# Soft mixture-of-experts on one core: products of one kind paired in every phase, and twenty-five pairs split a level deeper in place of nine

## The chip, the core and the metric

The kernel runs on one NeuronCore of a Trainium2 chip. The metric is the device time of one execution in microseconds (us). The profile is of one execution of the program; "span" is the time from its first to its last instruction in that profile, and the profiled execution's own time lies a little above it.

## The reference, cut to what matters

```python
# x (16, 512, 512), router_logits (16, 512, 8), expert_weights (8, 512, 2048), all f32
probs = softmax(router_logits, axis=-1)
for e in range(8):
    output += probs[:, :, e:e+1] * np.matmul(x, expert_weights[e])
```

With 8192 rows in all, this is one matrix product: on the left the 8 scaled copies of x side by side (8192 x 4096), on the right the experts' weights below each other (4096 x 2048).

## The kernel before, in words

**A fast product.** The kernel doesn't do the eight multiplications that a 2 x 2 by 2 x 2 block product has, but Winograd's seven, at two levels, and in some places three. At the outer level the rows go in blocks of 256; blocks a = 2q and b = 2q + 1 are a pair (q = 0 to 15), the experts are halved (0 to 3, 4 to 7) and the output's columns are halved (1024 each). This gives the seven products P1, P2, P5, P6, P7, P4 and P3, each for every q: `product(r, q)`. Each multiplies a left operand of 256 rows (some sum of x scaled by routing probabilities, made on VectorE by `times` and `less` in class `Left`) by a right operand (some sum of weight blocks, class `Right`), and adds the result into quarters of the output. `P1`, `P2` and `PQ` also name the three sets of probabilities in `p_dram`: first half of the experts, second half, and their sum.

At the inner level each product is again seven steps, `STEPS = (1, 5, 6, 2, 7, 3, 4)`. A step (`Product.step`) is 8 matmuls of 128 x 128 weights by 512 columns in float16 into a PSUM bank; `Product.post` then moves or adds the bank into f32 tiles `h` of 128 x 512 and sends a finished one out with a DMA. `post_alone` starts a result with ScalarE copies. `post_on_base` adds to a base, a tile read in beforehand: VectorE adds in six of the seven steps, ScalarE copies in step 2. Four h tiles make up the result of one product. The pool `hpool` has twelve, which also hold the `t5` copies below.

**A third level.** `run_third` does steps 1 and 5 of both products of a stage together, as seven parts each (class `Third`: sums `s` of the two left operands, made on VectorE; class `Split`: sums `t` of the right operand, made once, eight for the two steps). A part is 4 matmuls of 256 columns. So 56 matmuls of 256 columns stand in place of 32 of 512. After part 5 ScalarE copies half a bank to another bank and the other half to an h tile `t5` (L638 and L640), in that order, first for step 1 and then for step 5; VectorE adds `t5` back in parts 6 and 7. The last two steps of the stage before are held back and put between the parts (`held`).

**Stages.** `add` makes a stage of two products (the single (6, 0) and the last are alone). A stage has 14 slots, the steps of the two products by turns. There are 56 stages, 0 to 55: 0 to 3 have two P1 each; 4 to 9 one P2 and one P1; 10 to 14 two P2; 15 two P5; 16 to 30 P6 with P5; 31 is (6, 15) with (7, 0); 32 to 46 are P4 with P7; 47 is (4, 15) with (3, 0); 48 to 54 two P3; 55 the last P3. `k5`, `k7` and `k3` are 15, 31 and 47. Split are stages 2 and 3 (P1), 11 (P2), and 49 to 54 (P3).

**What sets the order.** All engines' instructions are kept in the order in which the Python code emits them. Hooks (`at(stage, slot, ...)`) put DMAs and weight work at a slot. VectorE's tasks wait in `queue`; `slack` runs them by a planner with two clocks, a slot of 1.73 us for TensorE (`SLOT`) and a cost for each task (0.69, 1.22 or 2.29 us), as far as VectorE's clock stays under TensorE's by `LAG`. `need` forces a task early when a step asks for it. `start_loads`, `store_loads` and `finish_loads` bring x and the probabilities for two stages later, at slots 1, 5 and 7; `late` moves the first for one stage.

**Queues.** SP's queue loads bases (`Base.fetch`), x and the probabilities, transposes x (L397), and stores x. POOL's queue casts weights and x from f32 (`cast_w`, `XBlock.begin`), writes results (`to_out`; for P4 and P3 with an accumulating DMA, `accum_op=ADD`), and stores made weights. ACT's queue, in order with ScalarE's copies, loads weights (`fetch_w`) and kept left operands (class `Operand`). Weight tiles are 1 MB; `wpool` has fifteen, which also hold the sums `s` and `t` and the operands.

**Bases and operands.** P6's left operand is stored for q in `KEEP` (1 to 13) and read again as a part of P3's. P7 makes its own from both x blocks (three passes for each half). P7 reads as its base what P6 wrote to the output; P4 takes P7's result as its base while that is still in h tiles, which is why the two share a stage. P2 does the same with P1's for q of 9 and more, and reads P1's stored result for smaller q.

**Weights in time.** `cast21`, `wedge`, `cast_odd` and `odd_t` make the sums of weight blocks for P2, P5 and P6 during stages 0 to 15; `by_parts` makes those of P7, P4 and P3 in quarters and stores them; `turnover` loads the seven right operands of P7, P4 and P3 over the last slots before they are used.

Of the kernel before, what the change touches and what calls it, by code (L numbers as in the profile page):

```python
# [31 lines left out]
def kernel(  # L32
# [340 lines left out]
    def evacuated(cost=0.69):  # L373
        clock["dve"] = max(clock["dve"], clock["pe"]) + cost
# [51 lines left out]
    class Left:  # L426
# [31 lines left out]
        def queue_make(self, k):  # L458
            for make in self.makes(k):
                self.task[k] = later(1.22, make)  # L460

        def queue_s2(self):
# [3 lines left out]
            self.task["s2"] = later(0.69, make)  # L466

        def queue_i(self):
# [5 lines left out]
            self.task["i"] = later(1.22, make)  # L474
# [19 lines left out]
    class Right:  # L494
# [9 lines left out]
        def queue_sum(self, sums, p):  # L504
            self.task[p] = later(2.29, sums[p])
# [66 lines left out]
    class Split:  # L572


        def __init__(self, right):
            self.right, self.t, self.task = right, {}, {}

        def queue(self):
            for p in THIRD:
                for i in range(4):  # L580
                    self.task[p, i] = later(0.69, lambda p=p, i=i: self.make(p, i))
# [18 lines left out]
    class Third:  # L600


        def __init__(self, a, b, split):
            self.a, self.b, self.split, self.task, self.s, self.t5 = a, b, split, [], None, {}

        def queue_sums(self):
            for i in range(4):
                self.task.append(later(0.69, lambda i=i: self.make(i)))

        def make(self, i):  # L610
            if i == 0:
                self.s = wpool.tile([P, 4, C, HQ], f16, name="s", tag="w")
            s, (a, b) = self.s, (p.left.t[0] for p in (self.a, self.b))
# [12 lines left out]
        def part(self, p, m):  # L626
# [14 lines left out]
            elif m in (6, 7):  # L641
                evacuated(0.42)
# [41 lines left out]
    right[1] = Right(w, {p: Task(2.29, sums[p]) for p in (6, 7, 4)})  # L684
    lefts, xs, ps_, bases = {}, {}, {}, {}
    KEEP = range(1, 14)
# [6 lines left out]
    def left_of(r, q, fresh=True):  # L693
# [15 lines left out]
        if r == 3 and q in KEEP:  # L709
            pt = PBlock(a, P2)  # L710
            return Left(xblock(a), pt, part=Operand(lefts[6, q].kept)), [xblock(a), pt]
# [6 lines left out]
    def product(r, q, **how):  # L718
# [7 lines left out]
        elif r == 2:  # L726
            if q >= 9:
# [21 lines left out]
        elif r == 4:  # L749
            p = Product(right[4], left, to_out(q, 1, 0, accum_op=ADD), products[7, q].o.__getitem__)  # L750
# [36 lines left out]
    def third(stage, r):  # L787
        if r not in splits:
            splits[r] = Split(right[r])
# [30 lines left out]
    def run_third(stage):  # L820
        t = thirds[stage]
        before(stage, 0)
        t.parts("x1", "x5", "q1", "q5")
# [4 lines left out]
        t.parts("x2", "q2", "x6", "q6")  # L828
# [4 lines left out]
        t.parts("x7", "q7", "x3", "q3", "x4", "q4")  # L833
        for p in THIRD:
            for product in (t.a, t.b):
                product.post(p)
        after(stage, 4)

    def run(stage):
# [3 lines left out]
        slots = [(p, i) for i in range(len(STEPS)) for p in some]  # L843
# [23 lines left out]
    for q in (2, 4, 6, 8):  # L867
        add(product(1, q), product(1, q + 1))
    for q in range(9, 15):
# [344 lines left out]
```

## Time and profile before

| | |
|---|---|
| runs, median (3) | 1382.1 us (1379.82 to 1384.07) |
| the profiled execution | 1378.23 us |
| its span | 1376.5 us |
| granted TensorE clock | 1.00 |
| VectorE busy | 1125.8 us, 1360 instructions |
| moved by DMA | 358.50 MB |

"A <- B: total, times, longest" tells who waited for whom. In the timeline a row is a run of equal instructions with its start, its length, and in brackets the idle time ahead of it and what ended that. In the view by stretches each engine has its busy time and count; the last three columns are the granted clock, the mean busy share of the sixteen DMA engines, and GB/s. The DMA share can be over 1, since packets overlap. A line number is often that of a helper: L132 is every matmul, L112 every VectorE sum, L123 SP's DMAs, L126 POOL's, L166 ACT's loads.

### The profile page before, as it was taken

The page shows a single profiled execution, that of the slowest core. Times are in us where ns is not written, and L with a number is a line of the kernel's source. Part 1 is how long each engine was busy: PE and PEld are TensorE (multiplying, and loading weights), DVE is VectorE, ACT ScalarE, POOL GpSimd, SP SyncE. Part 2 cuts the span into 40 slices and gives each one's busy share as a digit, 9 for nine tenths or more (in the row PEclk, how much of TensorE's full clock was granted, in tenths as well). Part 3 has the DMA queues.
Part 4 walks back from the last instruction along what each step waited for, and adds up shares of the span by engine and source line. Part 5 has one row for each costly group of instructions (what it writes and reads, how often), then busy time and mean ns, then how long its engine had stood idle before and what let it go on. Part 6 is the DMA issues. An engine that isn't in the chain of part 4 may idle for free.

```text
span 1376.5 us, 18061 instructions
## 1 busy us (share of the span) xinstructions
PE 1363.1 (99%) x6610; PEld 643.8 (47%) x6610; DVE 1125.8 (82%) x1360; ACT 193.3 (14%) x353; POOL 411.4 (30%) x652
## 2 busy tenths in 40 slices
PE   8999999999999999999999999999999999999998
PEld 4455444445444444444444444444444444456554
DVE  5877767678989888789897878888889898987875
ACT  3222111100001111111111100000000000123221
POOL 3122333231222243343242112232332422232222
PEclk9999999999999999999999999999999999999999
DMA  9999899999897999999999898888797969999886
GB/s 180 199 258 219 214 233 279 236 315 340 252 327 237 321 308 315 295 318 320 334 286 307 327 399 237 194 236 211 227 266 203 259 188 310 289 225 239 211 184 117
DMA packets 193161, 358.50 MB, mean 260 GB/s; under 512 B 53168, under 2 KB 87216, under 8 KB 187696
## 3 DMA queue, kind: packets, MB, share of 16 engines
q0 software_dynamic: 88688, 185.12, 55.7%
q1 hardware_dynamic: 98336, 130.15, 31.1%
q10 hardware_dynamic: 6048, 42.08, 8.0%
q8 instruction: 51, 0.84, 0.2%
q14 instruction: 38, 0.31, 0.1%
HBM read 214.47 MB, written 170.07 MB: 279 GB/s over the span
## 4 chain that ended last, share of the span: by engine, by line
PE 69%; issue 11%; DMA 11%; POOL 5%; DVE 3%; SPq 1%; ACT 0%; POOLq 0%; DVEq 0%; ACTq 0%
PE ps L132 69%; POOL out_dram L126 3%; DMA out_dram<-h 3%; DMA wd<-w 2%; DMA w<-in_expert_weights_dram 2%; DMA w<-wd 2%; DMA xT<-xs 1%; POOL wd L126 1%; DMA pT<-p_dram 1%; SPq L397 1%; DVE h L112 1%; POOL w L126 1%; DVE z L112 1%; DVE s L112 0%; POOL xs L126 0%
## 5 line engine op out<-in xcount | busy, mean ns | idle before, releaser
L132 PE MATMUL ps<-w,z 128*128 128x512 f16 (+1 forms) x5272 | 1136.0, 376 | 3.8 <-DMA w<-in_expert_weights_dram 1.9
L132 PEld LDWEIGHTS <-z 128*128 128x128 f16 x5344 | 522.6, 98 | 609.6 <-issue 2.5
L126 POOL DMA_DIRECT2D out_dram<-h x380 | 248.6, 660 | 724.1 <-ACT h L559 352.2
L112 DVE TENSOR_TENSOR h<-ps,h 128x512 f32<-128x512 f32 x415 | 284.7, 688 | 175.0 <-PE ps L132 147.0
L112 DVE TENSOR_TENSOR z<-xT,pT 128x2048 f16<-128x2048 f16 x220 | 266.8, 1218 | 12.1 <-DMA xT<-xs 10.0
L132 PE MATMUL ps<-w,d 128*128 128x512 f16 x880 | 199.1, 379 | 1.2 <-DMA w<-wd 1.2
L132 PEld LDWEIGHTS <-d 128*128 128x128 f16 x880 | 86.1, 98 | 103.3 <-issue 1.5
L112 DVE TENSOR_TENSOR z<-z,d 128x2048 f16<-128x2048 f16 x110 | 132.3, 1217 | 0.0
L112 DVE TENSOR_TENSOR w<-w 128x1024 f16<-128x1024 f16 (+2 forms) x92 | 101.0, 1103 | 5.9 <-DMA wd<-w 3.4
L559 ACT COPY h<-ps 128x512 f32<-128x512 f32 x64 | 37.5, 586 | 482.9 <-PE ps L132 414.2
L548 ACT COPY h<-ps 128x512 f32<-128x512 f32 x90 | 52.7, 586 | 325.6 <-PE ps L132 304.6
L112 DVE TENSOR_TENSOR ps<-ps,h 128x512 f32<-128x512 f32 (+1 forms) x102 | 60.6, 599 | 31.9 <-PE ps L132 31.8
L112 DVE TENSOR_TENSOR d<-z 128x1024 f16<-128x1024 f16 x110 | 74.8, 686 | 2.0 <-PE ps L132 0.7
L545 ACT COPY h<-ps 128x512 f32<-128x512 f32 x90 | 52.0, 589 | 151.7 <-PE ps L132 146.6
L126 POOL DMA_DIRECT2D w<-in_expert_weights_dram x65 | 48.4, 761 | 38.6 <-DMA wd<-w 28.3
L126 POOL DMA_DIRECT2D wd<-w x86 | 48.2, 584 | 37.1 <-DVE w L112 28.9
L126 POOL DMA_DIRECT2D kept<-h x56 | 30.8, 550 | 73.8 <-ACT h L548 41.1
L112 DVE TENSOR_TENSOR z<-z,u 128x2048 f16<-128x2048 f16 x38 | 46.4, 1221 | 0.6
L112 DVE TENSOR_TENSOR u<-xT,pT 128x2048 f16<-128x2048 f16 x38 | 46.3, 1217 | 0.0
L112 DVE TENSOR_TENSOR h<-h 128x512 f32<-128x512 f32 (+2 forms) x69 | 45.2, 676 | 0.4 <-DMA h<-kept 0.3
L541 ACT COPY ps<-ps 128x512 f32<-128x512 f32 x45 | 25.6, 570 | 104.5 <-PE ps L132 99.4
L112 DVE TENSOR_TENSOR z<-z 128x2048 f16<-128x2048 f16 x32 | 39.1, 1222 | 0.6
(61 smaller groups left out, 262.5 us busy)
## 6 DMA issues: line engine op xcount, KB each, us to landing
out_dram<-h POOLq DMA_DIRECT2D x380, 256.0 KB, 6.7
pT<-p_dram SPq DMA_DIRECT2D x127, 256.0 KB, 6.3
w<-wd ACTq DMA_DIRECT2D x27, 1024.0 KB, 9.4
h<-kept SPq DMA_DIRECT2D x100, 256.0 KB, 7.1
xT<-x SPq DMA_DIRECT2D x74, 256.0 KB, 6.6
wd<-w POOLq DMA_DIRECT2D x72, 256.0 KB, 6.7
w<-in_expert_weights_dram POOLq DMA_DIRECT2D x35, 512.0 KB, 9.9
h<-out_dram SPq DMA_DIRECT2D x68, 256.0 KB, 4.8
```

The lines of the kernel that those rows point to most:

```text
L112: dve(nc.vector.tensor_tensor(out=o, in0=a, in1=b, op=op))
L126: note(nc.gpsimd.dma_start(out=o, in_=i, **how))
L132: note(nc.tensor.matmul(ps, z, w, start=start, stop=stop, skip_group_check=True))
L397: note(nc.sync.dma_start_transpose(out=self.t[:, :, ds(j * P, P)], in_=self.xs[:, j, :]))
L541: act(nc.scalar.copy(self.banks["b"], x))
L545: act(nc.scalar.copy(o[tn], q if p == 5 else x))
L548: act(nc.scalar.copy(o[TN[p]], b if p == 2 else x))
L559: act(nc.scalar.copy(o[tn], b))
```

## The change

Products of one kind now stand in one stage together. Stages 0 to 6 have two P1 each, 7 to 14 two P2, 15 to 31 are as they were, 32 to 38 have two P7, 39 is (7, 15) with (4, 0), 40 to 46 have two P4, and the rest is as it was. `k2` is 7 and `k4` is 39. So P4's result can't find P7's in h tiles, and reads it back from the output; P2 reads P1's stored result for q up to 13. P7's left operand is x of block b times `P2` less P6's kept one, for q of 1 to 14 (`KEEP` is one longer). Split are 2 to 6 (P1), 8 to 11 (P2), 33 to 37 (P7, step 1 alone), 41 to 45 (P4), and 49 to 54 (P3) as before. The weights of P4 and P3 are loaded in the one stage before their first use, every second slot. Casts and sums of weights for P2, P5 and P6 get other slots, and block (1, 1) of P5's and P6's is made from whole casts. The loads of x and probabilities start at slot 6 in stages 32 to 46. The planner's costs are lowered. The last product does step 3 before 7 and step 2 in two halves around step 4, both copied by ScalarE.

```diff
-    def evacuated(cost=0.69):
+    def evacuated(cost=0.61):
...
-        def __init__(self, right):
-            self.right, self.t, self.task = right, {}, {}
+        def __init__(self, right, ps):
+            self.right, self.ps, self.t, self.task = right, ps, {}, {}
...
-    KEEP = range(1, 14)
+    KEEP = range(1, 15)
...
-        if r == 3 and q in KEEP:
-            pt = PBlock(a, P2)
-            return Left(xblock(a), pt, part=Operand(lefts[6, q].kept)), [xblock(a), pt]
+        if q in KEEP and (r == 7 or r == 3 and q < 14):
+            h = a if r == 3 else b
+            pt = PBlock(h, P2)
+            return Left(xblock(h), pt, part=Operand(lefts[6, q].kept)), [xblock(h), pt]
...
-            if q >= 9:
+            if q >= 14:
                 base = products[1, q].o.__getitem__
...
-            p = Product(right[4], left, to_out(q, 1, 0, accum_op=ADD), products[7, q].o.__getitem__)
+            base = bases[4, q] = Base(lambda tn: out_rows(q, 1, 1, tn))
+            p = Product(right[4], left, to_out(q, 1, 0, accum_op=ADD), base)
...
     def run_third(stage):
         t = thirds[stage]
+        both = len(t.split.ps) == 2
+        some = ("x1", "x5", "q1", "q5", "x2", "q2", "x6", "q6") if both else ("x1", "x5", "x2", "x6")
         before(stage, 0)
-        t.parts("x1", "x5", "q1", "q5")
+        t.parts(*some[:4] if both else some[:2])
...
-    for q in (2, 4, 6, 8):
+    for q in range(2, 16, 2):
         add(product(1, q), product(1, q + 1))
-    for q in range(9, 15):
-        add(product(2, q), product(1, q + 1))
...
-    rest = [15] + list(range(9))
-    for i in range(0, 10, 2):
+    rest = [14, 15] + list(range(14))
+    for i in range(0, 16, 2):
         k = add(product(2, rest[i]), product(2, rest[i + 1]))
...
-    for q in range(15):
-        add(product(4, q), product(7, q + 1))
+    for q in range(1, 15, 2):
+        add(product(7, q), product(7, q + 1))
+    some = product(7, 15)
+    xs.clear()
+    k4 = add(some, product(4, 0))
+    for q in range(1, 15, 2):
+        add(product(4, q), product(4, q + 1))
...
+    for stage in range(k7 + 1, k3):
+        late[stage] = 6
...
+    for r, first in ((7, k7 + 1), (4, k4 + 1)):
+        for slot, tn in zip((8, 10, 12, 13), INNER):
+            for q in range(16):
+                if (r, q) != (7, 0):
+                    k = first + (q - 1) // 2
+                    fetch_at(k if tn == (1, 0) else k - 1, 3 if tn == (1, 0) else slot, bases[r, q], tn)
...
-    for i, kn in enumerate(((0, 0), (0, 1), (1, 1), (1, 0))):
-        at((11 * i + 8) // 14, (11 * i + 8) % 14, lambda kn=kn: cast21(kn))
+    for where, kn in zip([(3, 10), (4, 7), (5, 4), (5, 13)], ((0, 0), (0, 1), (1, 1), (1, 0))):
+        at(*where, lambda kn=kn: cast21(kn))
...
+    for q, where in zip((12, 11, 22), [(7, 4), (7, 10), (8, 2), (8, 12)]):
+        at(*where, lambda q=q: cast_odd(q, (1, 1)))
+    at(*(8, 12), lambda: odd_t((1, 1)))
...
-    by_parts(k7 + 4, 4, 36, 3, cast_part(22), keep_raw, (9, 16))
+    by_parts(k7 + 2, 4, 36, 3, cast_part(22), keep_raw, (9, 16))
...
-    turnover(k7, 0, 4, "t4")
-    turnover(k3 - 1, 1, 3, "b22")
+    for r, raw, stage in ((4, "t4", k4 - 1), (3, "b22", k3 - 1)):
+        turnover_of(r, raw, [(stage, 1 + 2 * i) for i in range(7)])
...
-    finish.steps = (1, 5, 6, 7, 3, 4, 2)
+    finish.steps = (1, 5, 6, 3, 7, "2a", 4, "2b")
...
-    for stage in (2, 3):
+    for stage in [2, 3, 4, 5, 6]:
         third(stage, 1)
-    at(1, 2, splits[1].queue)
-    for stage in (11,):
+    at(1, 0, splits[1].queue)
+    for stage in [8, 9, 10, 11]:
         third(stage, 2)
-    at(10, 2, splits[2].queue)
+    at(k2, 2, splits[2].queue)
...
+        at(k7 - 1 + (q - 1) // 2, 8 + 3 * ((q - 1) % 2), lambda q=q: lefts[7, q].part.fetch())
...
+    for r, stages_ in ((7, [2, 3, 4, 5, 6]), (4, [2, 3, 4, 5, 6])):
+        for stage in stages_:
+            third((k7 if r == 7 else k4) + stage, r, *([(1,)] if r == 7 else []))
+        if stages_:
+            at((k7 if r == 7 else k4) + stages_[0] - 1, 2, splits[r].queue)
```

In the changed file the copies of the split stand at L639 and L641.

## The prediction

> **What bounds the kernel now.** I read the page first, then who TensorE waited for, then its timeline, then the transfers and VectorE by stage.
>
> ```profile
> span 1376.5 us, 18061 instructions
> PE 1363.1 (99%) x6610; PEld 643.8 (47%) x6610; DVE 1125.8 (82%) x1360; ACT 193.3 (14%) x353; POOL 411.4 (30%) x652
> ```
>
> TensorE is busy for 99% of the span. The profile calls that no proof of a full engine, since matmuls are pipelined, so I take the waits and the start-to-start times.
>
> ```profile
> PE ps L132 <- DMA w<-in_expert_weights_dram: 1.9, 1, 1.9
> PE ps L132 <- DVE h L112: 1.5, 2, 0.8
> PE ps L132 <- ACT h L331: 1.4, 1, 1.4
> PE every L94 <- DVE zero L91: 1.3, 1, 1.3
> PE ps L132 <- DVE t L112: 1.3, 1, 1.3
> PE ps L132 <- DMA w<-wd: 1.2, 1, 1.2
> PE ps L132 <- DVE s L112: 1.0, 1, 1.0
> PE ps L132 <- ACT ps L638: 0.3, 1, 0.3
> PE ps L132 <- DVE ps L112: 0.2, 1, 0.2
> ```
>
> Columns: us in total, times, longest. All of TensorE's waits come to 10.1 us. Those for expert weights, L331 and zero (4.6 us) lie in the prologue, which stays as it is. The rest is 5.5 us: 1.5 + 1.3 + 1.2 + 1.0 + 0.3 + 0.2. So the time is the sum of the matmuls, and only fewer matmul columns or fewer waits can shorten it.
>
> ```profile
> 198.97 14.41 PE L132 MATMUL ps<-w,z 128*128 128x512 f16 x66
> ...
> 1216.94 2.76 PE L132 MATMUL ps<-w,z 128*128 128x512 f16 x16
> ...
> 1240.32 2.76 PE L132 MATMUL ps<-w,z 128*128 128x512 f16 x16
> ```
>
> The columns are start, us, and how many in a row; the last matmul's pipeline adds about 0.16 us to each row. 66 matmuls of 512 columns take 14.41 us, or 0.216 us each. A stage of two unsplit products has 112 of them: 24.18 us. The other two rows mark the same place in two split stages that follow each other (49 and 50): 23.38 us for 80 matmuls of 512 and 56 of 256 columns. 80 x 0.2159 is 17.27, so one of 256 columns takes 0.109 us, half of the long one and 1 ns.
>
> **The change part by part.**
>
> *More split pairs.* A full split puts 56 short matmuls in place of 32 long ones: 24.18 - 23.38 = 0.80 us. Before has nine; after has twenty full ones (5 of P1, 4 of P2, 5 of P4, 6 of P3) and five of P7 that split step 1 alone: 28 short for 16 long, 3.45 - 3.06 = 0.40 us. Eleven more full and five half: 8.8 + 2.0 = **10.8 us less** on TensorE, on the path that sets the end.
>
> *Old waits.* P1's halves are queued two slots earlier (DVE ps and one DVE h); P2 and P1 no longer share stages 4 to 9, and stage 11 is no longer the first split of P2; P4's weights no longer wait for P6's tiles (DMA w<-wd); the next left operand of the last split is planned in time; the last product does step 3 before step 7. I let all **5.5 us** go, and then ask what is late next.
>
> *First splits on new bases.* In before the first P2 split stood still here:
>
> ```profile
> 308.75 0.60 PE L132 MATMUL ps<-t,s 128*128 128x256 f16 x4 [1.26 <-DVE t L112]
> 311.86 0.60 PE L132 MATMUL ps<-w,z 128*128 128x256 f16 x4 [0.35 <-ACT ps L638]
> ```
>
> Its eight weight combinations on VectorE came late. In after the stage ahead of the first split of P2 and of P4 (7 and 40) has 25.7 us of VectorE work for 25.9 us of TensorE, and that of P7 (32) 25.1 for 25.05. The rates are start to start:
>
> ```profile
> 195.19 2.35 DVE L112 TENSOR_TENSOR z<-xT,pT 128x2048 f16<-128x2048 f16 x2
> 197.47 0.68 DVE L112 TENSOR_TENSOR h<-ps,h 128x512 f32<-128x512 f32 x1
> 198.06 0.68 DVE L112 TENSOR_TENSOR d<-z 128x1024 f16<-128x1024 f16 x1
> 198.66 1.22 DVE L112 TENSOR_TENSOR z<-xT,pT 128x2048 f16<-128x2048 f16 x1
> ```
>
> They give 0.60 us for an eviction or a 1024-column sum and 1.13 for a 2048-column one. Three such places at 0 to 1.3 us; I take half: **1.9 us**.
>
> *The copy's tile.* The second wait is another thing. The split's ScalarE copy into `t5` needs an h tile, of which there are twelve, and a product with a base holds four. The tile was still being written out:
>
> ```profile
> 311.16 0.37 ACT L640 COPY h<-ps 128x256 f32<-128x256 f32 x1 [3.66 <-DMA out_dram<-h]
> ```
>
> ```profile
> 294.26 1.53 POOL L126 DMA_DIRECT2D w<-in_expert_weights_dram x2 [0.21 <-PE ps L132]
> 298.46 0.57 POOL L126 DMA_DIRECT2D out_dram<-h x1 [2.67 <-ACT h L559]
> ```
>
> ```profile
> 298.46 12.62 DMA out_dram<-h
> ```
>
> The write took 12.62 us behind two 512 KB casts in POOL's queue. ScalarE is in order, so the copy for the other half (L638), and with it TensorE, waited behind it. In after, P2's, P7's and P4's fourteen splits all have bases, and the same tile order: from the write of step 2 to the copy lie five steps and two parts, 5 x 1.73 + 0.87 = 9.5 us. The median write takes 6.7 us (last fence below), so most pass. Two have casts just ahead (slot 4 of stages 7 and 33, write in slot 6). Each costs between 0 and the 0.35 + 1.26 = 1.6 us that this one would have cost without the wait beside it: **3.2 us**; the other end is all nine full ones of P2 and P4, 14.4 us.
>
> *VectorE in P7.* Taking x_b P2 minus the kept operand saves one pass per k half, 28 x 1.13 = 32 us of VectorE over the phase. But P7 and P4 apart load it unevenly: a half-split P7 stage has 12 evictions (7.2), 10 wide sums (11.3), two s2 (1.2), four half sums (1.2), two short adds (0.7), plus about 1.2 of weight sums: 22.8 to 23.2 of 23.78 us.
>
> ```profile
> 1098.00:1122.00 24.00, 24.00 (x113) 10.92 (x112) 22.21 (x27) 1.17 (x2) 6.38 (x11) 1.00 0.80 207
> ```
>
> At 22.21 us busy in 24.00 before lost nothing; at 97% for five stages there is 0.6 to 1 us a stage left. Ends: 0 and 1 us a stage; I take **1.0 us** in all, nearest that row.
>
> *Transfers.* Added reads: P4's base (64 x 256 KB, 16.8 MB), five more P2 bases (5.2), fourteen operands (14.7); with smaller items after moves 393 MB for 358.5. Added issues: SP 64 + 20 base loads, ACT 14 operand loads ahead of its copies. What they lie beside is TensorE; what they do to each other shows where before turned weights over:
>
> ```profile
> 782.00:806.30 24.30, 24.30 (x113) 10.85 (x112) 21.22 (x26) 1.77 (x3) 4.86 (x9) 1.00 1.01 396
> 806.30:831.90 25.60, 24.38 (x114) 10.98 (x113) 19.72 (x24) 1.17 (x2) 4.02 (x7) 1.00 1.01 371
> 164.40:188.60 24.20, 24.20 (x113) 10.97 (x112) 16.85 (x20) 3.50 (x6) 8.25 (x15) 1.00 0.96 250
> 1240.30:1263.70 23.40, 23.40 (x139) 13.34 (x138) 18.95 (x25) 6.96 (x15) 6.82 (x9) 1.00 0.94 229
> ```
>
> The last three columns are clock, share of the DMA engines and GB/s. 396 GB/s was had for a whole stage, full. After asks 13.6 MB of stage 38 (seven 1 MB weights for P4, 2.1 MB of bases, 2.1 of writes, 1.05 of x and p, 1.05 of casts), 7.1 of stage 39, and 12.9 of stage 46. 20.7 MB over 48.4 us at 396 GB/s is 52.3, 3.9 us too long; the weights are issued 24 us ahead of use. Before lost 1.2 us at such a place. I take that twice: **2.4 us** (ends 0 and 27, below).
>
> What the queues do to each other there:
>
> ```profile
> q10 hardware_dynamic: 788, 5.73, 57.3%
> q1 hardware_dynamic: 1067, 1.96, 23.3%
> q0 software_dynamic: 589, 1.91, 20.5%
> ...
> w<-wd ACTq DMA_DIRECT2D x5, 1024.0 KB, 13.2
> out_dram<-h POOLq DMA_DIRECT2D x9, 256.0 KB, 9.5
> h<-out_dram SPq DMA_DIRECT2D x5, 256.0 KB, 11.7
> ```
>
> ```profile
> out_dram<-h POOLq DMA_DIRECT2D x380, 256.0 KB, 6.7
> h<-out_dram SPq DMA_DIRECT2D x68, 256.0 KB, 4.8
> ```
>
> The weights (q10, issued by ACT) held 57% of the engines while the urgent base loads on SP went from 4.8 to 11.7 us. The Trainium skill ("DMA: Bandwidth & Descriptors", Queues, rings and completion order) says that an engine goes round the queues packet by packet; by that rule early weights do slow the bases, and the trace agrees (57.3, 23.3 and 20.5%). The same page's Specifications give about 358 GB/s of HBM per core; by that, an estimate, the 20.7 MB would take 57.8 us, 9.4 too long; the row at 396 stands against it as a limit. The sum goes by the rows.
>
> *What I cost at nothing.* The base for step 6 is fetched at the start of a split stage, 4 to 7 us after the write that frees its tile, and first read 9 to 12 us later. SP waits there, with the next bases and x and p behind it (these now start at slot 6, not 1, in stages 32 to 46, still 22 us or more ahead of their first read); VectorE's add waits, with evictions behind it; TensorE needs that add only at step 7, four steps (6.9 us) later. That cover is gone if bases take the 11.7 us above and the write 9.5: then 1 to 3 us of VectorE a stage, which P7 can't make up. The third sums for (1, 1), made from whole casts in place of two wedges, add 3 x 2.2 us of VectorE in stages 8 and 9, beside TensorE (22.4 us of work for 23.4). The casts moved into stages 3 to 5 feed sums three and more stages later; they lie beside TensorE unless x behind them in POOL's queue is late. The planner's costs (0.61 and 1.14) now meet the rates above; they shift VectorE's order, not its work. At the end one half copy goes from VectorE to ScalarE; after the last matmul stand one copy and one 128 KB store as before.
>
> **The sum.** -10.8 - 5.5 + 1.9 + 3.2 + 1.0 + 2.4 = -7.8 us against the profiled execution: 1378.2 us, that is the span and 1.7 around it. 1378.2 - 7.8 = 1370.4. The median of the runs, 1382.1, stands 3.9 above that execution, so 1374.3: **1374**.
>
> **Rivals.** *All is covered:* no new waits, -16.3: 1366. For it: nothing waits in stages 49 to 52, splits without a base. Against: the bases.
>
> *The copy's tile everywhere:* all nine full splits of P2 and P4 pay 1.6 us, 14.4 in place of 3.2: 1385.5. For it: writes at 9.5 us median in a full stage use up the whole 9.5 us of room. Against: 6.7 us overall.
>
> *The transfers become the bound (slower).* Price: the weights at q10's 57.3% of 24.3 us for 5.73 MB, 2.43 us a MB: 17.8 us for 7.3 MB. In stage 38 the other 6.3 MB at the 2.75 us a MB of q1 and q0 (43.8% of 24.3 for 3.87) is 17.3: 35.1 of 24.2, 10.9 over. In stage 46 the other 5.5 MB, half accumulating writes, at 4.1 us a MB (the row 1240, 229 GB/s at 0.94) is 22.6: 40.4, 16.2 over. All 27 on TensorE is 1374.3 - 2.4 + 27.1 = 1399; half, 1385; I name 1392. It decides when weights land over 24 us after issue, or SP's bases over some 17 us; 13.2 and 11.7 were the medians before. Stages 3 and 4 add to its chance: 7.9 MB of casts and writes at 260 GB/s (250 at 0.96) need 30 us of 23.4.
>
> *The split saves nothing:* excluded by 23.38 against 24.18.
>
> **How the numbers follow.** Forecast case (1368 to 1380) 0.40; all covered 0.15; tile everywhere 0.18; transfers 0.27. About 0.3%, 4.1 us, can be told from no change: under 1378.0 is faster, over 1386.2 slower. Faster: 0.15 + 0.37 = 0.52. Same: 0.03 of the forecast case, 0.14 of the tile case, 0.03 of transfers: 0.20. Slower: 0.04 + 0.24 = 0.28. Range 1363 to 1394: it leaves out some 0.05 below and 0.12 of the transfers case above. The forecast case's own range is 1368 to 1380.
>
> **What would show it.** Right: TensorE's matmul starts in a split P4 stage 23.4 us apart; new waits on DVE t and on L639/L641 of 1 to 2 us each in stages 8, 34 and some P4 splits; w<-wd waits under 3 us. Wrong: waits of TensorE over 15 us in all; bases (h<-out_dram) landing above 15 us in stages 38 to 47; VectorE lag growing from stage 33 to 37; or a span under 1363.

## The result, and the profile after

The changed kernel is slower: 1413.14 us median (1410.55 to 1419.24, four runs) against 1380.96 beside it, a ratio of 1.0247 [1.0220, 1.0273]. The forecast was 1374, its range 1363 to 1394. The profiled execution of after took 1419.24 us, its span is 1417.5; that of before is 1376.5, so 41.0 us are to be explained. The medians differ by 32.2: after's profiled execution is the longest of its four, and before's (1378.23) is shorter than its four beside them. Medians and ranges are of all runs of a kernel; two kernels below have one run each (1398.0 and 1402.24) more than 1.5% above their fastest, which the ratios leave out.

First the page, the same two lines as of before:

```profile
span 1417.5 us, 19121 instructions
...
PE 1368.7 (97%) x6934; PEld 679.0 (48%) x6934; DVE 1151.0 (81%) x1458; ACT 210.7 (15%) x408; POOL 409.8 (29%) x650
```

TensorE went from 99% to 97% busy. Who it waited for:

```profile
PE ps L132 <- DVE ps L112: 18.8, 6, 8.6
PE ps L132 <- DVE h L112: 12.4, 8, 4.7
PE ps L132 <- ACT h L641: 3.2, 1, 3.2
PE ps L132 <- ACT ps L639: 3.0, 1, 3.0
PE ps L132 <- DMA w<-in_expert_weights_dram: 1.9, 1, 1.9
PE ps L132 <- DMA w<-wd: 1.6, 1, 1.6
PE ps L132 <- DVE t L112: 1.5, 2, 1.0
```

The matmuls themselves did what was forecast. Stages that don't stop take 23.4 us with a full split and 23.8 with a half one, against 24.2; by the starts of all matmuls the change saves 10.7 us. Everything else is stops. Here is the time beyond 0.2159 us from the start of one matmul of 512 columns to the next (0.1092 for 256), summed by place:

| stages | before | after | what was late |
|---|---|---|---|
| 5, 6 | 0 | 12.0 | x |
| 10, 11 | 1.9 | 5.3 | t5's tile |
| 22, 23 | 0 | 4.8 | sums of P4's weights (code as before, planner's costs new) |
| 31, 32 | 1.5 | 3.0 | P7's first weight, P7's `t` |
| 34 | 0 | 6.2 | t5's tile |
| 39 | 0 | 6.6 | bases of (4, 0), (4, 1) |
| 40 to 45 | 0 | 4.5 | bases |
| 46, 47 | 0 | 14.8 | bases of (4, 14), (4, 15) |
| others | 3.6 | 1.3 | |

That is 58.5 for 7.0, and 51.5 - 10.7 = 40.8 us.

**What differs from one execution to another.** One execution of each kernel was profiled. So I counted the same places in the profiles of the experiments below. Where an experiment leaves their code as it is, stages 5 and 6 stop for 3.6 to 8.1 us (six profiles), against 12.0 here, and 22 and 23 for 0 to 6.3 (seven), against 4.8. Stages 39, 46 and 47 together stop for 15.7 to 22.9 in the six kernels that keep P4's base and the bytes of its and P3's weights, against 21.4. The last is the steady part, and some of the 9 us between 41 and 32 is probably the long stop of stage 5.

**The clock.** Not all of it is waiting. This is the timeline around the stop in stage 34:

```profile
868.81 2.33 PE L132 MATMUL ps<-w,z 128*128 128x512 f16 x12
874.31 1.01 PE L132 MATMUL ps<-t,s 128*128 128x256 f16 x4 [3.17 <-ACT h L641]
875.12 3.62 PE L132 MATMUL ps<-w,z 128*128 128x512 f16 x8
878.53 1.06 PE L132 MATMUL ps<-t,s 128*128 128x256 f16 x4
```

Eight matmuls of 512 columns take 3.62 us there in place of 1.89: they run at half clock. The trace grants TensorE 0.5 behind each stop of 2.5 us or more, 37.5 us in all. In after TensorE stood for 40.4 us (5.6 in before, both without the prologue) and lost 13.8 to the slow clock, half of the 27.5 us that it was busy in those stretches (none in before); most of the remaining 4 us is the 0.16 that each of some twenty restarts takes.

**The DMA engines.** The view by stretches, first before (stages 33 to 45), then after (33 to 45):

```profile
831.90:1146.10 314.20, 314.20 (x1457) 142.42 (x1456) 275.07 (x329) 15.23 (x26) 102.46 (x151) 1.00 0.86 226
```

```profile
846.80:1174.00 327.20, 316.02 (x1638) 161.26 (x1637) 275.55 (x376) 24.54 (x54) 100.00 (x149) 0.98 1.03 296
```

Before had a seventh of the engines' time to spare through P7 and P4. After has none, for 300 us on end: more bytes in each stage (P7's kept operand; P4's base, read back), and on top of them the weights of P4 (stage 38) and P3 (stage 46). The transfers became slower, as these rows of the whole run show (before's medians were 6.7 and 4.8):

```profile
out_dram<-h POOLq DMA_DIRECT2D x380, 256.0 KB, 8.1
h<-out_dram SPq DMA_DIRECT2D x132, 256.0 KB, 9.2
```

A share of about 1 does not stop TensorE by itself. In before's stages 15 to 30 the engines had it too, with TensorE busy all the time:

```profile
407.30:782.00 374.70, 374.70 (x1738) 169.86 (x1737) 320.81 (x393) 54.88 (x94) 121.49 (x216) 1.00 1.00 305
```

So the share tells where there is no room for more, and the waits tell what is late. The longest stop, stage 47, in the chain of waits (start, us, what):

```profile
1185.94 14.57 DMA pT<-p_dram
...
1200.52 0.02 SPq L123
...
1200.57 16.78 DMA h<-out_dram
...
1217.44 0.71 DVE ps L112
...
1218.19 3.95 PE ps L132 x10
```

A base is issued at 1200.57 only when a load of probabilities issued 14.6 us before has landed, takes 16.8 us itself, and VectorE, which is in order and had waited for it for 12.9 us, then lets TensorE go on. Why SP waits there is in the last section.

### The profile page after: what moved, and what is told of

The parts are those of the page before. It is cut to its first block, busy times and chain, and to the rows that moved or that the text cites. A ratio compares the mean times of both kernels' runs of the same rounds, so it can differ in the third digit from the quotient of the medians.

```text
span 1417.5 us, 19121 instructions
## 1 busy us (share of the span) xinstructions
PE 1368.7 (97%) x6934; PEld 679.0 (48%) x6934; DVE 1151.0 (81%) x1458; ACT 210.7 (15%) x408; POOL 409.8 (29%) x650
## 5 line engine op out<-in xcount | busy, mean ns | idle before, releaser
L132 PE MATMUL ps<-w,z 128*128 128x512 f16 (+1 forms) x5056 | 1085.0, 373 | 18.9 <-DVE h L112 12.4
L132 PEld LDWEIGHTS <-z 128*128 128x128 f16 x5236 | 514.3, 98 | 594.2 <-issue 38.2
L112 DVE TENSOR_TENSOR h<-ps,h 128x512 f32<-128x512 f32 x415 | 280.6, 685 | 138.8 <-PE ps L132 95.7
L132 PE MATMUL ps<-w,d 128*128 128x512 f16 x880 | 202.3, 383 | 8.6 <-DVE ps L112 8.6
L112 DVE TENSOR_TENSOR ps<-ps,h 128x256 f32<-128x256 f32 (+1 forms) x156 | 80.8, 536 | 55.3 <-PE ps L132 36.1
L112 DVE TENSOR_TENSOR w<-w 128x1024 f16<-128x1024 f16 (+2 forms) x91 | 102.9, 1137 | 10.7 <-DMA wd<-w 5.8
L132 PE MATMUL ps<-t,s 128*128 128x256 f16 x540 | 75.6, 275 | 5.8 <-ACT h L641 3.2
L132 PEld LDWEIGHTS <-s 128*128 128x128 f16 x720 | 70.9, 99 | 21.3 <-issue 8.1
L112 DVE TENSOR_TENSOR z<-z,o 128x2048 f16<-128x2048 f16 x54 | 65.8, 1218 | 1.2 <-DMA o<-kept_left 0.5
L126 POOL DMA_DIRECT2D wd<-w x84 | 46.4, 564 | 54.4 <-DVE w L112 27.5
L639 ACT COPY ps<-ps 128x256 f32<-128x256 f32 x45 | 16.1, 358 | 187.1 <-PE ps L132 179.9
## 6 DMA issues: line engine op xcount, KB each, us to landing
o<-kept_left ACTq DMA_DIRECT2D x27, 1024.0 KB, 10.1
```

The source lines that it names most:

```text
L112: dve(nc.vector.tensor_tensor(out=o, in0=a, in1=b, op=op))
L126: note(nc.gpsimd.dma_start(out=o, in_=i, **how))
L132: note(nc.tensor.matmul(ps, z, w, start=start, stop=stop, skip_group_check=True))
L639: act(nc.scalar.copy(ya[:, COLS[0]], yb[:, COLS[0]]))
```

## The experiments

All times are medians in us; the kernel before, run beside each, gave 1379.1 to 1381.4.

**A stop and its clock.** An addition to the kernel before (`still` is a tile of its own):

```diff
             p.step(p.steps[i])
+            if stage in LADDER and n == 3:
+                mm(p.banks["q"], still[:, 0:P], p.right.op(5)[:, 0, :], False, True)
...
             p.post(p.steps[i])
+            if stage in LADDER and n == 2:
+                for j in range(LADDER[stage]):
+                    act(nc.scalar.mul(still, still if j else p.banks["q"][:, 0:HQ], 0.0))
```

> Kernel before with one more matmul (a zero operand, so that nothing is added) in each of stages 17, 19, 21, 23, 25, 27 and 29; it waits for a chain of 6, 8, 10, 12, 14, 18 and 24 small ScalarE operations that starts when step 5 of the stage's first product ends. TensorE then stands for 0 to some 7 us at seven places. Theory (a stop of about 3 us or more halves TensorE's clock for 3.4 us after it): the short stops cost their own length, those of over some 2.5 to 3 us cost 1.7 us or more beside it, with the granted clock at 0.5 in the 3.4 us behind them; the whole is the sum of the stops plus 1.7 for each of the long ones. Rival (the slow clock in the changed kernel has another cause, such as busy DMA): clock 1.0 throughout, each stop costs its length.

The span is 1434.3, 57.8 longer; the seven stops are 42.7 of it, one of 1.71 and six of 4.05 to 10.45. The second in the timeline, and the stretches beside it:

```profile
503.65 0.61 PE L132 MATMUL ps<-w,still 128*128 128x512 f16 x1 [4.09 <-ACT still L857]
504.05 5.84 PE L132 MATMUL ps<-w,d 128*128 128x512 f16 x16
```

```profile
503.65:507.06 3.41, 3.41 (x9) 1.21 (x10) 0.00 (x0) 0.58 (x1) 1.28 (x3) 0.50 1.12 329
...
508.70:512.00 3.30, 3.30 (x17) 1.51 (x16) 3.27 (x4) 0.93 (x2) 0.00 (x0) 1.00 1.21 290
```

Nine matmuls in 3.41 us at clock 0.50, then seventeen in 3.30 at 1.00. The short stop left the clock at 1.00. The other six lost 12.5 us to it, 2.1 each: the theory holds, the price is a little higher than it said. Another stop, of 3.0 us in stage 32 and not of the ladder's making, left the clock at 1.00 too. So a stop of 4 us or more cost its length and about 2 us, and one between 2 and 4 us may or may not pay them; the last section says when.

**Half of the change alone.** The stages, bases, weights and splits of P7 and P4 put back to those of before:

```diff
-    for q in range(1, 15, 2):
-        add(product(7, q), product(7, q + 1))
...
+    for q in range(15):
+        add(product(4, q), product(7, q + 1))
...
-        if q in KEEP and (r == 7 or r == 3 and q < 14):
+        if q in KEEP and r == 3:
...
-    for r, stages_ in ((7, [2, 3, 4, 5, 6]), (4, [2, 3, 4, 5, 6])):
```

> P1 and P2 apart as in the changed kernel, with the changed last product and costs; P7 and P4 as before (alternating, unsplit, P4 on P7's values, no operand kept for P7). Theory (each stop has a cause near it): the stops of stages 5 and 11 stay with 17 us, those of stages 32 to 47 go; six more split pairs than before are 4.8 us less: 1381 + 17 - 4.8 - 3 of old waits = 1388 to 1393. Rival (P7's and P4's part is a gain that P1's stops hide): slower than 1404.

1384.27 (1380.08 to 1394.57), a ratio of 1.0035 [1.0011, 1.0059]. That is 4 us under the theory's range. By subtraction, of the 32 us 29 belong to P7 and P4, and P1's and P2's part costs 3. Its profiled execution (span 1391.5) is one of two long ones among the ten: it stops for 11.2 us in stage 5, 4.9 in 10 and 11, 5.2 in 22, 4.3 in 32, and for no more than 0.4 in any other. So the stops of stages 33 to 47 go with P7's and P4's part, and those of 5 and 11 stay, as the theory says; most runs of this kernel are some 9 us shorter than the one that shows them.

**The planner.**

```diff
-    def evacuated(cost=0.61):
+    def evacuated(cost=0.69):
...
-            self.task[p] = later(2.2, sums[p])
+            self.task[p] = later(2.29, sums[p])
```

(and all the other costs of before)

> Changed kernel with the planner's costs of before (0.69, 1.22, 2.29 in place of 0.61, 1.14, 2.20; 0.42 for 0.35): the same instructions, VectorE's order more cautious. Theory (late transfers cause the stops): the stops in stages 5, 11, 34, 39 and 46 to 47 stay, time 1407 to 1420. Rival (VectorE planned with no margin): the waits of TensorE for VectorE, 32 us in all, halve: 1385 to 1397.

1418.73 (1415.03 to 1419.77): the rival is out; the lower costs are no loss. The time is the theory's, the places only in part: 5 (7.9) and 47 (15.5) stop, but 34 doesn't, 11 only for 2.4 and 39 for 1.0, and others come in their place (5.4 in 10, 5.0 in 38). TensorE now waits 13.5 us for operands (`DVE z`), which the new costs had put earlier.

**What the turnovers cost.**

```diff
     def turnover_of(r, raw, places):
-        right[r].w = {}
...
+        right[r].w = right[7].w
```

> Changed kernel in which P4 and P3 use P7's weights, so that the fourteen 1 MB weight loads of stages 38 and 46 are left out (the results of P4 and P3 are then of other weights). Theory (weights loaded in a burst of one stage hold up the bases on SP and each other): the stops of stage 39 (6.6 us with the slow clock) and of 46 and 47 (14.8 us) go, bases there land in under 8 us: 1391 to 1395. Rival (SP waits for h tiles and writes, weights or not): both stay, 1408 to 1414. Rival (all bytes count): half goes, about 1402.

1386.54 (1376.97 to 1398.0), 26.6 less. Stages 39, 46 and 47 have no stop left; in after's profile they had 21.4. The rest of the 26.6 isn't assigned: in this profile stages 5, 6, 22, 23 and 34, which the edit leaves alone, stop for less as well. In stages 38 and 39 bases landed in 7.9 us and writes in 6.3, where after has these (four of the seven weights are issued inside the stretch), and this share and rate for the two stages:

```profile
out_dram<-h POOLq DMA_DIRECT2D x20, 256.0 KB, 10.8
h<-out_dram SPq DMA_DIRECT2D x16, 256.0 KB, 13.6
w<-wd ACTq DMA_DIRECT2D x4, 1024.0 KB, 9.0
```

```profile
973.50:1028.50 55.00, 50.25 (x226) 22.35 (x225) 39.95 (x50) 2.25 (x4) 18.53 (x31) 0.97 1.04 357
```

The weights themselves land in 9.0 us; it is the bases and writes beside them that become late. That leaves open whether weights as such are too much, or only weights on top of full engines. So the bytes under them were taken away, and the weights left:

```diff
-            base = bases[4, q] = Base(lambda tn: out_rows(q, 1, 1, tn))
-            p = Product(right[4], left, to_out(q, 1, 0, accum_op=ADD), base)
+            p = Product(right[4], left, to_out(q, 1, 0, accum_op=ADD))
...
-    for r, first in ((7, k7 + 1), (4, k4 + 1)):
+    for r, first in ((7, k7 + 1),):
```

> Changed kernel in which P4 leaves out the base: P7's values are neither read back nor added to P4's results (four VectorE adds of a product become ScalarE copies). P4's stages move 2.1 MB less each; the weight loads stay. Theory (the DMA engines are full in P7 and P4, and whatever comes on top stops TensorE): the stops of stages 46 and 47 (14.8 us) and of 40 to 45 (4.5) go, that of 39 (6.6) by half or more: 1388 to 1396. Rival (the weight loads stop TensorE by themselves): the stops of 46 and 47 stay, 1405 to 1413.

1391.56 (1386.96 to 1396.96), 21.6 less. Stages 40 to 47 have no stop at all, with the seven weights still loaded in 46. The engines have room in 41 to 45 (first row) and are full in 46 and 47 for two stages, which cost nothing:

```profile
1037.80:1156.40 118.60, 118.60 (x682) 66.54 (x681) 77.63 (x103) 34.71 (x70) 42.36 (x53) 1.00 0.88 161
1156.40:1180.60 24.20, 24.20 (x113) 10.98 (x112) 15.80 (x17) 5.83 (x10) 6.90 (x9) 1.00 1.04 311
1180.60:1204.80 24.20, 24.20 (x114) 10.96 (x113) 21.84 (x26) 5.83 (x10) 6.95 (x9) 1.00 1.06 314
```

The stop of stage 39, behind P7 whose bytes stayed, is still there (8.9), against the theory's half. It has full stages ahead of it and more room behind it (0.88). Before's turn to P7 is placed alike, between 1.00 and 0.86, and cost only 1.2 us; what makes the difference stays open. VectorE is also relieved in this kernel, so it doesn't separate bytes from VectorE's load. The next one comes nearer to that: the kernel before, all its instructions in place, with added copies.

```diff
+    for k in range(k7 + 1, k3):
+        for i in range(2):
+            at(k, 4 + 7 * i, lambda i=i, k=k: note(nc.scalar.dma_start(out=junk[i], in_=x_f[ds(((k * 2 + i) % 8) * 2 * HQ, 2 * HQ), :])))
```

> Kernel before with two 1 MB copies from x to an unused place in DRAM added on ScalarE's queue in each of the stages 32 to 46, about the bytes that the change adds there. Theory (full DMA engines): the share of the engines goes from about 0.85 to 1.0 in these stages, and the turnover to P3 in 46 and 47, which cost nothing, now stops TensorE, as does that of 32: 1390 to 1405. Rival (the order of loads and tiles in the pairs of one kind is at fault, not the bytes): 1380 to 1385.

1403.78 (1399.97 to 1412.18), 22.9 more than before, a ratio of 1.0175 [1.0141, 1.0209]. Stages 32 to 46, and the waits:

```profile
807.40:1171.70 364.30, 343.37 (x1569) 154.41 (x1568) 293.36 (x352) 16.32 (x28) 106.74 (x157) 0.97 1.00 301
```

```profile
PE ps L132 <- DVE h L112: 18.4, 5, 10.1
PE ps L132 <- DVE ps L112: 9.6, 3, 7.8
```

About the share and GB/s of after, and stops of 10.7 us in stage 33, 11.8 in 44 and 8.2 in 47, with the two of 44 and 47 in VectorE's adds that wait for h tiles still being written (11.2 and 8.3 us). TensorE waits for no copy of ScalarE there, on whose queue the added copies stand. In stage 33 VectorE waits 12.6 us for a base that takes 19.2 to land. Over the same stages the writes land in 11.8 us (median) in place of 6.4, the bases in 8.2 in place of 4.9. So pairs of P4 and P7 stop as well once more is moved beside them: neither the new order nor the splits are needed for it. The copies also take turns on the completion semaphores that SP's loads use (last section); the late writes of 44 and 47 are POOL's and don't. Where the stops fall differs from after; the copies go from DRAM to DRAM and are not the same packets.

**Can the weights be arranged better?**

```diff
-        turnover_of(r, raw, [(stage, 1 + 2 * i) for i in range(7)])
+        turnover_of(r, raw, [(stage + (4 * i - 9) // 14, (4 * i - 9) % 14) for i in range(7)])
```

> Changed kernel with P4's and P3's seven weight loads issued every four slots from slot 5 of the stage before (37 and 45) to slot 1 of stages 39 and 47, in place of every two slots of one stage: the same bytes over 43 us in place of 21. Theory (a burst that other transfers wait behind): bases land in under 10 us there, most of the 21 us of stages 39, 46 and 47 goes: 1394 to 1402. Rival (the total of bytes): at most a third goes, 1406 to 1413. Rival (a weight waits for its tile on ScalarE's queue and holds up the copies behind it): slower than 1413.

1410.84 (1410.22 to 1417.39): 2 us less, the rival of the bytes. Stage 39 stops for 8.5, 46 and 47 for 14.4. Spreading a burst over stages that are as full buys nothing here.

```diff
-                right[r].w[p] = fetch_w(raw, RAW[p])
+                what = raw, RAW[p]
...
+            right[r].w[p] = new_w()
+            pool(right[r].w[p], stored[what])
```

> Changed kernel with the fourteen weight loads of P4 and P3 issued by POOL in place of ScalarE, at the same slots: the same bytes at the same time, but they no longer take completion semaphores that SP's loads also use, and they share POOL's queue with the writes. Theory (SP's bases are held by semaphores and by a third queue): SP's bases land earlier, in under 9 us, and the stops of 39 and 47 shrink by half or more, 1399 to 1406, unless the writes behind the weights come to over 17 us, which frees h tiles late and keeps the stops. Rival (bytes alone): 1410 to 1416, bases as late as before.

1405.02 (1400.16 to 1406.92), 8 less. The time is in the theory's range, the stops are not halved: in the profile 39 stops for 11.3, 46 not at all, 47 for 8.3, 19.6 in place of 21.4. That is within what other profiles show there (15.7 to 22.9), and stage 5 alone stops for 6 us less, so the 8 can't be put down to the queue. SP's bases of stages 38 and 39 landed in 10.1 us, sooner than 13.6, not under 9, and VectorE waited there for a store of weight parts as well (7.4 us). The queue and its semaphores are at most the smaller part.

**The other stops.**

```diff
-    for where, kn in zip([(3, 10), (4, 7), (5, 4), (5, 13)], ((0, 0), (0, 1), (1, 1), (1, 0))):
+    for where, kn in zip([(4, 2), (4, 10), (5, 4), (5, 13)], ((0, 0), (0, 1), (1, 1), (1, 0))):
...
-    for (kn, e), (where, then) in zip(((kn, e) for kn in ((0, 0), (1, 0)) for e in range(2)), [((1, 2), (1, 13)), ((2, 4), (3, 1)), ((3, 6), (4, 3)), ((4, 8), (5, 5))]):
+    for (kn, e), (where, then) in zip(((kn, e) for kn in ((0, 0), (1, 0)) for e in range(2)), [((1, 2), (1, 13)), ((2, 4), (3, 1)), ((3, 4), (4, 3)), ((4, 8), (5, 5))]):
```

> Changed kernel with three casts moved: the wedge of stage 3 from slot 6 to slot 4, and the block casts of stages 3 and 4 from slots 10 and 7 to slots 2 and 10 of stage 4, so that in POOL's queue x for stage 6 no longer stands behind them; the bytes of stages 3 to 5 stay. Theory (order in POOL's queue): x lands within 10 us of issue, the 8.35 us stop in stage 5 and its half-clock time go, -10 to -12 us: 1401 to 1403. Rival (VectorE too tight): VectorE still waits for nothing that matters, the stop stays, time within 3 us of 1413. Rival (too many bytes in these stages): x lands as late as before, or the sums of P2's weights do, and at least 6 of the 12 us stay.

1405.93 (1401.17 to 1411.8), 7 less. First after, who VectorE waited for around stage 5, and TensorE's stop:

```profile
DVE z L112 <- DMA xT<-xs: 9.7, 1, 9.7
```

```profile
175.80 1.86 PE L132 MATMUL ps<-t,z 128*128 128x256 f16 x8 [8.35 <-DVE ps L112]
```

Now the same place with the casts moved:

```profile
170.45 1.64 PE L132 MATMUL ps<-t,z 128*128 128x256 f16 x8 [1.96 <-DVE ps L112]
```

The cast of x now lands 7.4 and 7.6 us after its issue in place of 12.6 and 13.1, but the transposes behind it take 13.0 to 17.2 in place of 9.0 to 16.0. The stop of stage 5 is 4.5 with its clock, from 11.6. Stage 7 has a new one of 4.9: VectorE waited 3.7 us for the last cast (issued at 202.96, landed at 215.62) and then for x of stage 8. So 9.4 us of stops are left, which is the third expectation: too many bytes in these stages (share 1.20 and 1.17 in 4 and 5). How much the order in POOL's queue is worth isn't shown. With the casts where they were, POOL issued x at 149.0 us in after, at 146.2 in the run with a tile of its own for `t5`, and at 138.6 to 141.3 in five other runs; the stops of stages 5 and 6 were 12.0, 8.1 and 3.6 to 5.9. So the stop goes with late x, and with the same code it can be as short as with the casts moved.

```diff
-                self.t5[n] = h_tile([P, HQ], f32)
+                if self.right_no == 1:
+                    self.t5[n] = h_tile([P, HQ], f32)
+                else:
+                    if not self.t5:
+                        self.own = zpool.tile([P, 2, HQ], f32, name="u", tag="u", bufs=1)
+                    self.t5[n] = self.own[:, "xq".index(n)]
```

> Changed kernel in which the split's second copy (t5) of P2, P7, P4 and P3 goes to a tile of its own (the one named u, idle there) in place of one of the twelve h tiles. Theory (ScalarE waits there for an out write behind casts): the stops of stage 11 (5.3 us with the slow clock) and stage 34 (6.2) go, and two h tiles more per split help the bases of P4 too: 1398 to 1403. Rival (the copy is only the first to show a late write, the base of step 6 waits next): 1407 to 1413, with DVE h waits in place of the ACT ones.

1407.12 (1401.6 to 1408.41), 6 less: the rival's time. Both waits for ScalarE are gone, and stage 34's stop with them (2.2 to 5.0 us there in five other profiles with P7's splits and after's costs). In stage 11 a stop of 3.8 is left: VectorE waits 6.6 us there for a base (`h<-kept`). Half theory, half rival.

```diff
-    for r, stages_ in ((7, [2, 3, 4, 5, 6]), (4, [2, 3, 4, 5, 6])):
+    for r, stages_ in ((7, []), (4, [])):
```

> Changed kernel with P7's and P4's pairs left unsplit: the same transfers, five stages longer by 0.8 us and five by 0.4 (6.0 us of TensorE), no t5 and no weight sums on VectorE there. Theory (transfers): the stops of stages 39, 46 and 47 stay with 15 to 21 us, that of 34 goes: 1408 to 1414. Rival (the splits' work on VectorE makes it late): all stops in P7 and P4 go, 1386 to 1394.

1400.01 (1397.8 to 1402.25), 13 less, though TensorE has 6 us more to do: between the two. Stops in 39 (4.6) and 47 (11.1) stay, as the theory says; those in 34, 37 and 40 to 46 go, as the rival says, and 38 gets 1.5. In stages 40 to 45 VectorE is busy for 0.65 to 0.76 of the time without splits and for 0.75 to 0.93 with them. So, by the medians, the splits of P7 and P4 saved 6 us and cost some 19 (by the profiles' stops from stage 33 on, some 16). They take VectorE's slack and h tiles that had hidden late bases; which of the two counts for more isn't separated.

**Towards a faster kernel.** P1's and P2's part alone with both repairs (the last cast in slot 10 of stage 5):

> P1 and P2 apart with P7 and P4 as before (as in the run that did that part alone, 1384.3), and with both repairs: the casts of stages 3 to 5 as in the run that moved them (the last of them at slot 10 of stage 5 in place of 13), and the t5 copy of P2's and P3's splits in the tile named u. Theory (each stop has its cause near it): the two repairs gave 7 and 6 us on the whole changed kernel, of which the parts in P1 and P2 are 5 to 8 and 2 to 4: 1372 to 1378, under before. Rival (a stop repaired comes back some stages on): 1380 to 1386.

1383.89 (1375.36 to 1402.24, six runs), a ratio of 1.0014 [0.9977, 1.0051]: no difference, the rival's number. The profiled execution (span 1376.2, near the lowest) has no stop of over 0.5 us in stages 0 to 10; 11 and 12 have 3.6, 22 and 23 4.8, 32 2.4. Two more (the sums in `by_parts` 19 slots behind their loads; the old costs):

```diff
-    by_parts(*slots_after(k5 + 2, 4, 60), 24, 4, load_p4, less_t2, (8, 15))
+    by_parts(*slots_after(k5 + 2, 4, 60), 24, 4, load_p4, less_t2, (8, 19))
```

> The repaired P1/P2 kernel (1383.9) with the sums of P4's weight parts queued 19 slots behind their loads in place of 15, so that they stand further behind the stores of the same parts. Theory (VectorE waits in stage 22 for a store issued just ahead of the sums): the stop of stages 22 and 23 (4.8 us in the profile) goes, 1377 to 1380. Rival (writes are late there whatever the order): 1382 to 1386.

> The repaired P1/P2 kernel with the planner's costs of before (0.69, 1.22, 2.29). Theory (the stop of stage 22, in a part that the change leaves alone, comes from the new costs, which put the sums of the parts right behind their stores): it goes, 1377 to 1380, if the operands of P1's and P2's splits are still in time. Rival (the new costs save VectorE's work from being late in the splits): waits on DVE z and ps in stages 5 to 12 take its place, 1384 to 1392.

1386.24 (1377.72 to 1392.21, twelve runs) and 1391.49 (1382.44 to 1398.33): both theories fail, and the rivals' times came, the first to 0.2 us. The stop of stages 22 and 23 is gone in the first profile and 1.7 in the second. That doesn't show that the sums stood too close behind their stores, since it is 0 to 0.4 too in four profiles with the order of after (without the turnover's weights, without P4's base, with unsplit pairs, with casts moved). It buys nothing: the first stops for 6.7 us in stage 4, 4.3 in 7 and 6.5 in 32, the second for 6.4 in stage 6, 5.1 in 10 and 5.1 in 32. No version beat the kernel before. What differs from run to run in these kernels, by 14 to 17 us (without the 1402.24) where before beside them keeps within 10, stays open; the stops that move about are in it, but only one execution of each was profiled.

## Why the prediction was wrong

**More split pairs, -10.8:** right, 10.7.

**Old waits, -5.5:** most went, but 1.6 for `w<-wd` is still there, one stage earlier.

**First splits' `t`, +1.9:** 1.5 by the wait for `DVE t`. Right.

**The copy's tile, +3.2:** too small. The mechanism was right (a write behind casts, ScalarE in order). Two places paid, stage 34 as named and 11 in place of 8, but 3.0 and 3.2 us each for the 1.6 taken, and 11.1 with the slow clock. The cap of 1.6 came from a place where another wait ran beside it and the stop stayed short.

**VectorE in P7, +1.0:** stages 33, 35, 36 and 37 lost 0.8. Right as long as its data were there.

**Transfers, +2.4: this is the step that failed.** It took the 1.2 us of before's turnover twice. The turnovers cost 21.4 us in the profile, 15.7 to 22.9 in six others, and 26.6 by the medians of the run without their weights. The prediction had counted the demand (20.7 MB for stages 38 and 39) and found 3.9 us too much of it, and then took its price from a turnover that had a seventh of the engines' time to spare in the stages behind it (0.86). After has none (1.03), so what didn't fit in had no later place to go; with more bytes in those stages before stopped for 10.7 us just behind its own turn to P7. Room behind isn't all of it, as stage 39 without P4's base shows. The best rate of one stage, 396, was taken as the rate to be had; stages 38 and 39 ran at 357, and 46 and 47 at 297. The Trainium skill gives about 358 ("DMA: Bandwidth & Descriptors", Specifications), which the prediction had set aside; the 396 over one stage stands, so here it is no ceiling. The kernels without the weights, without P4's base and with added copies show that what moves beside a turnover makes it stop; a rule for when full engines cost time isn't shown.

**Costed at nothing.** The casts in stages 3 to 5 were "beside TensorE unless x behind them in POOL's queue is late". It was, and that was 12.0 us in this execution, 3.6 to 8.1 in others; the prediction had the 30 us of bytes for 23.4 in hand, among the reasons for the slower rival, and left it out of the sum. The late bases it described came: 4.5 us in stages 40 to 45. The stop of stage 22 (4.8) wasn't thought of. The prediction said that the new costs "shift VectorE's order, not its work"; whether the order makes this stop isn't shown.

**The clock.** No term knew that a long stop is followed by half clock: 13.8 us, a part of the figures by place above. The Trainium skill has the rule ("TensorE: Matmul & The Clock Gate", Part 1: The HAM clock gate: after an idle window of about 3.4 us the array runs at half rate). The ladder agrees that half clock follows, at 2.1 us a stop; in the runs less idle time is enough (last section). Before had no stop long enough to show it.

**The rivals.** The one that ended slower had the right cause and nearly the right price: 10.9 and 16.2 us for two turnovers that cost 6.6 and 14.8 in the profile. Its condition came true for SP's bases (up to 19.7 us, for the 17 named), not for the weights (9 us). Its time, 1392, was half of that price put on a sum that left out x, the slow clock and stage 22. It deserved more than 0.27, since two places (stages 3 to 5 and 38) had more bytes on the table than time. Of the signs named, the wrong ones came (40.4 us of waits, bases above 15 us), and of the right ones the 23.4 us of a split P4 stage.

## What to carry to other kernels

Count the bytes of each stage against the rate of that stage's kinds of transfers, over the whole phase and not only at its peak: seven weights loaded at a turnover cost 1.2 us in before, with room behind, and 6.6 and 14.8 in after, where the stages around were full. A gain of 0.8 us a stage that takes the last slack of VectorE and of the buffers is worth less than that slack once transfers are late. Price a stop of TensorE at its length and the slow clock behind it. Before a stop is put down to its neighbour, see whether it stands in another execution of the same code.

## What the runs showed of the hardware

**When the clock halves.** The slow stretches of a trace are whole multiples of 3.413 us and lie on one grid, whatever the kernel does. I summed TensorE's idle time in each window of that grid, over the fifteen profiles of the changed kernel and the experiments, without their prologues. Of 294 windows at full clock with some idle time, every one with 2.08 us or more of it was followed by a window at half clock (52 windows), and none with 1.94 or less (237); of five between, two were. Once at half, 0.93 us of idle in a window kept it there and 0.64 didn't. So a stop of 2.4 us costs nothing more if it is cut by the grid (1.01 and 1.41 in one run of the spread weights) and 1.6 us more if it isn't (stage 11 with the casts moved). The Trainium skill ("TensorE: Matmul & The Clock Gate", Part 1: The HAM clock gate) says that the window is 3413 ns and free-running. The grid agrees; the 2 us are from the runs.

**Transfers take turns on eight semaphores.** In the traces of before and after all DMAs of SP and ACT signal one of eight semaphores, those of POOL one of eight others, and none is issued before the one ahead of it on the same semaphore has landed. In after 113 of 636 on SP's and ACT's eight are issued within 0.3 us of that landing, in before 33 of 544. This is how these programs are built; whether the chip asks for it isn't shown. At 14 to 17 us for a transfer, as in the chain above, an in-order queue then issues slowly, and an urgent base waits for a load that nobody needs yet.

**Bytes are not alike.** With the engines full, a stage of P7 moved 340 GB/s, and one of P4, with accumulating writes, 215 (its five split stages together 243). That the accumulating is the reason isn't separated here. The two stages:

```profile
900.50:924.30 23.80, 23.80 (x125) 12.15 (x124) 23.49 (x32) 1.82 (x4) 5.41 (x11) 1.00 1.01 340
...
1051.60:1075.10 23.50, 23.50 (x139) 13.25 (x137) 21.97 (x34) 2.26 (x5) 11.57 (x15) 1.00 1.11 215
```
